# Another order for the filling work under the top-k search, and other steps for the down product's sums

## The chip, the cores and the metric

One core of a Trainium2 chip runs the whole kernel. The metric is the device time of one execution in microseconds (us); the profile is one further execution, read on the engines' own clocks.

## What is computed

One layer of a decoder trunk on x of 1024 tokens by 1024 channels, all in float32:

```python
h = x @ w_in + b_in                        # split into two groups of heads
A = sliding_window_attention(h)            # 8 q heads, 2 kv heads, window 128, sinks
B = sparse_attention(h)                    # indexer scores, top 256 keys, latent attention
x = LN(alpha * x + concat(A, B) @ w_o)
x = LN(alpha * x + cross_attention(x, mem))   # 4 heads over 256 memory tokens
x = LN(alpha * x + relu(x @ w_up) ** 2 @ w_down)
```

## The kernel before

A float32 product is made of three products on PE (TensorE), high by high, high by low and low by high. Each operand is split first: the high part is a rounding copy (ACT or POOL), the low part a subtraction (POOL or DVE, L166 and L1189).

**The fill.** From 149 us on, DVE and ACT search each row's threshold for the top 256 scores, and then DVE writes the masks (`mask_rows`, L820 to L830), 30 operations in six groups. PE has no part in this, so a list `fill` of other units is emitted beside it. A *projection* (`proj_unit`) is 24 products of 128x512 on the transposed x: ka (2 halves), qa (8), qb (8). Its result is split by ACT and DVE (L437, L438) and stored to DRAM by SP (L445). The other units: `mem_t` transposes the memory tokens; `lat` loads a latent weight and `latent_k` multiplies it (3 products); `mem_k` and `mem_v` are 24 products of 128x256 each; `mem_vo` multiplies by the output weight (12 products of 128x512 in each half). Each weight is loaded by SP into a ring of four raw tiles `wr`, split into a ring of four `wh`/`wl`. `open_attention` ends the life of the transposed x; the attention's operands (`KA`, from `first_loads`, L399) are put in its place, so no such load can be issued ahead of the last projection. The units before `CUT` are emitted ahead of `settle_all`, a branch that DVE takes after it has read a flag (`odd_row`, L754); the others follow it.

**The orders.** A scheduler fixes each engine's list of instructions when the program is built. An engine runs its list strictly in order, and SP issues loads and stores in its order too: a store that waits for DVE holds back every load behind it.

**The down product.** 28 of 32 row blocks of `w_down` are multiplied in a Strassen-like scheme of seven steps on quarters A11 to A22 and B11 to B22. `CHUNKS` runs three of them: 4 block pairs in the form `BACK`, 4 in `ONWARD`, 6 in `BACK`. A step's tuple names the sums of quarters it makes (DVE, L1435), the two quarters that it multiplies, and the additions of its results into `xr` (DVE, L1382, `out_add`). Of each pair of operands the high parts are copied by ACT (L1188) and the low parts are subtracted by DVE, or by POOL for three in eight (`lo_engine`, L1189). `AHEAD` keeps a sum from running more than five of DVE's subtractions ahead. The last four blocks are plain products, whose operands `in_slots` loads and splits (L1460 to L1462) into the places of quarters that are done.

Of the kernel before, what the change touches and what calls it, by code (L numbers as in the profile page):

```python
# [21 lines left out]
P = 128  # L22
KT = D // P
# [12 lines left out]
NOSYNC = mybir.DependencyInfo(mybir.DependencyClass.NoSync, mybir.DependencyReason.DATA)  # L36
# [3 lines left out]
def kernel(ctx: ExitStack, tc: tile.TileContext, x, mem, ln_emb_g, ln_emb_b, w_in, b_in,  # L40
# [449 lines left out]

    def mem_proj(c):
        if c % 2 == 0:
            FW["w"] = wload(xa_wkv, 0, KT, c * P, 256, lo=(POOL, DVE))
        wh, wl = cols(FW["w"], c % 2 * P)
        p = fill_bank()
        mm3(p[:, :M], [(wh[k], wl[k], memT[k // 4][:, k % 4, 0], memT[k // 4][:, k % 4, 1]) for k in range(KT)])
        return p[:, :M]
# [78 lines left out]
                W2[0] = qa, W2["bt"], qb, [bias_parts(e) for e in range(2)]  # L576

    qa, qb = [], []
    small = [(mem_t, mt, g) for mt in range(2) for g in range(2)] + [(lat, "uk", dsa_w_uk)]
    small += [(latent_k, j, t0, n) for j in range(4) for t0, n in HALVES] + [(lat, "uv", dsa_w_uv)]  # L580
    small += [(mem_k, c) for c in range(4)]
    heavy, fill = fill, []
    done = 0
    for i, u in enumerate(heavy):
        fill.append(u)
        want = i * len(small) // (len(heavy) - 1)
        fill += small[done:want]
        done = want
    fill += [(mem_k, c) for c in range(4, KT)]
    for h in range(4):  # L590
        fill += [(mem_v, h, d) for d in range(2)]
        if 0 < h < 3:
            fill += [(mem_vo, h - 1, nh) for nh in range(2)]
    fill.append((move_v,))
    for at, u in zip((13, 11, 10, 9, 8, 6, 5), [(open_attention,)] + [(first_loads, i) for i in range(6)]):
        fill.insert(len(fill) - at, u)

    CUT, MASKS = 26, 20
    ik = kdup(p1, ik_d, ("ikh",), ("ikl",))
    cm = p1.tile([P, P], F32, name="cm")  # L600
    DVE.memset(cm, 0.0)
# [231 lines left out]
    for unit, *args in fill[:CUT]:  # L833
        unit(*args)
    settle_all()
    for i, (unit, *args) in enumerate(fill[CUT:]):
        if i == MASKS:
            mask_rows()
        unit(*args)
    behind.clear()  # L840
    s1.close()
# [76 lines left out]
    def values(h0):  # L918
        vv = p2.tile([P, NB, 4, P], F32R, name="VV", bufs=1)
        us = slice(h0 * 64, h0 * 64 + 256)  # L920
        for s in range(0, NB, 2):
            p = psum.tile([P, 2, 256], F32, name="mm", bufs=2)
            for i in range(2):
                ts_ = slice((s + i) * P, (s + i) * P + P)
                mm3(p[:, i], [(cT[:, 0, ts_], cT[:, 1, ts_], uvh[:, us], uvl[:, us])])
            p_h = p.rearrange("p s (h d) -> p s h d", h=4)
            ACT.activation(vv[:, s:s + 2, :, 0:64], p_h, AF.Copy)
            DVE.tensor_tensor(out=vv[:, s:s + 2, :, 64:P], in0=p_h, in1=f(vv[:, s:s + 2, :, 0:64]), op=OP.subtract)
        return vv
# [327 lines left out]
    for j in range(1, NPRE):  # L1257
# [13 lines left out]
    A, B = OP.add, OP.subtract  # L1271
    ONWARD = (
        ((("B21", "B21", A, "B22"),), "A12", "B21", ((0, 0, A),), ()),
        ((("B12", "B12", A, "B11"),), "A21", "B12", ((1, 1, A),), ()),
        ((("AZ", "A11", A, "A22"), ("A21", "A21", A, "AZ")), "A21", "B11", ((1, 0, A), (1, 1, B)), ("A21",)),
        ((("A12", "A12", A, "AZ"),), "A12", "B22", ((0, 1, A), (0, 0, B)), ("A12",)),
        ((("B11", "B11", A, "B22"),), "AZ", "B11", ((0, 0, A), (1, 1, A)), ("AZ", "B22")),
        ((("B12", "B12", B, "B11"),), "A11", "B12", ((0, 1, A), (1, 1, A)), ("A11", "B12")),
# [1 line left out]
    BACK = (  # L1280
        ((("B21", "B21", B, "B11"),), "A22", "B21", ((0, 0, A), (1, 0, A)), ()),
        ((("B12", "B12", B, "B22"),), "A11", "B12", ((0, 1, A), (1, 1, A)), ()),
        ((), "A12", "B22", ((0, 1, A), (0, 0, B)), ()),
        ((), "A21", "B11", ((1, 0, A), (1, 1, B)), ()),
        ((("A11", "A11", A, "A22"), ("B11", "B11", A, "B22")), "A11", "B11", ((0, 0, A), (1, 1, A)), ("A22", "B22")),
        ((("A21", "A21", B, "A11"), ("B12", "B12", A, "B11")), "A21", "B12", ((1, 1, A),), ("A21", "B12")),
        ((("A12", "A12", B, "A11"), ("B21", "B21", A, "B11")), "A12", "B21", ((0, 0, A),), ("A12", "B21", "A11", "B11")))
    LOADS = {ONWARD: (("A12", "B21", "B22"), ("A21", "B12", "B11"), ("A11", "A22")),
             BACK: (("A22", "B21", "B11"), ("A11", "B12", "B22"), ("A12", "A21"))}

# [112 lines left out]
    for c, (r0, nk, steps) in enumerate(CHUNKS):  # L1403
        R, more, tags = {}, {}, {}

        def quarter(nm):

            t = free.pop(0)
            tags[nm] = [t]
            t = big(t, (P, 4, 512), F32)  # L1410
            R[nm] = [t[:, n] for n in range(4)]
            if nk > 4:
                pair = next(q for q in SHARED if nm in q)
                if pair not in more:
                    t = free.pop(0)
                    more[pair] = big(t, (P, 2, 2, 512), F32)
                    tags[pair] = [t]
                R[nm] += [more[pair][:, pair.index(nm), n] for n in range(2)]

        for names in LOADS[steps]:  # L1420
            for nm in names:
                quarter(nm)
            for n in range(nk):
                for nm in names:
                    SP.dma_start(R[nm][n], quarter_src(nm, r0 + 2 * n + int(nm[2 if nm[0] == "A" else 1]) - 1))
        if steps is ONWARD:
            quarter("AZ")
        for s, (sums, a, b, outs, done) in enumerate(steps):
            joined, open_ = c > 0 and s == 0, s == len(steps) - 1
            if not joined:  # L1430
                ps = [psum.tile([P, 512], F32, name=t, tag=t) for t in HALF[nst % 2]]
                nst += 1
            for n in range(nk):
                for o, x, op, y in sums:
                    i = DVE.tensor_tensor(out=R[o][n], in0=R[x][n], in1=R[y][n], op=op)  # L1435
                    if len(on_dve) > AHEAD:
                        tc.add_manual_dep(i.ins, on_dve[-1 - AHEAD].ins.name, NOSYNC, reason="order")
                ab = []
                for nm, w in ((a, WH), (b, WL)):
                    t = place(pw, w, [P, 2, 512], F32R)  # L1440
                    eng = lo_engine()
                    i = split(t, R[nm][n], eng)
                    if eng is DVE:
                        on_dve.append(i)
                    ab.append(t)
                for i in range(4):
                    ts_ = slice(i * P, i * P + P)
                    mm3(ps[i], [(ab[0][:, 0, ts_], ab[0][:, 1, ts_], ab[1][:, 0], ab[1][:, 1])],
                        n == 0 and not joined, n == nk - 1 and not open_)
            if not open_:  # L1450
                for i in range(4):
                    for t, d, op in outs:
                        out_add(ps[i], t * 4 + i, d, op)
            free += [t for q in (*done, *(q for q in more if set(q) <= set(done))) for t in tags[q]]
# [65 lines left out]
```

## Time and profile before

| | |
|---|---|
| median of three runs | 1546.09 us (1544.24 to 1546.13) |
| the profiled execution | 1550.19 us, its span 1548.4 us |
| PE busy | 1439.8 us (93%), mean granted clock 0.976 |
| PE weight loads | 1201.2 us (78%) |
| DVE, ACT, POOL busy | 1074.5 (69%), 754.0 (49%), 783.0 us (51%) |

A busy share is an average over all stages; a stage's own limit is read from the windows and the timelines of that stage. PE's clock is given as a share of full speed: 1.00 is 2.4 GHz, 0.50 is 1.2 GHz.

### The profile page before, as it was taken

How to read it: one execution, taken by the hardware profiler on the slowest of the kernel's cores; microseconds unless marked ns; L12 is line 12 of the kernel's file. 1: busy time of each engine (PE TensorE's matmuls, PEld its weight loads, DVE VectorE, ACT ScalarE, POOL GpSimd, SP SyncE). 2: the span in 40 equal slices, each digit the busy share in tenths (PEclk: the TensorE clock that was granted, in tenths of full speed). 3: DMA queues.
4: the chain of work that ended last, by engine and by line, in shares of the span. 5: the costliest groups of instructions: out<-in, count | busy, mean ns of one | idle time of the engine just before them, and what ended most of it. 6: DMA issues, size and time to landing. Idle time of an engine off the chain costs nothing. (4 is left out here: it accounts for less than half of the span.)

```text
span 1548.4 us, 21760 instructions
## 1 busy us (share of the span) xinstructions
PE 1439.8 (93%) x7190; PEld 1201.2 (78%) x7190; DVE 1074.5 (69%) x2060; ACT 754.0 (49%) x1517; POOL 783.0 (51%) x714
## 2 busy tenths in 40 slices
PE   4989998889989998999999889999999999999887
PEld 3977876768878876788888678888888877887676
DVE  6639888337769859883453775655444999978857
ACT  6437723447768844345153254455554543444422
POOL 6213433335548637566456575454443344354745
PEclk9999999989999999999999989999999999999899
DMA  6252544885595377333222134333334932410012
GB/s 220 67 166 62 164 123 131 281 267 149 160 262 161 113 227 225 123 109 107 85 83 89 41 116 150 103 123 109 109 109 157 374 104 95 155 55 0 28 35 102
DMA packets 140049, 206.62 MB, mean 133 GB/s; under 512 B 18199, under 2 KB 83230, under 8 KB 139934
## 3 DMA queue, kind: packets, MB, share of 16 engines
q1 hardware_dynamic: 139934, 205.21, 42.1%
q8 instruction: 57, 0.93, 0.3%
q14 instruction: 58, 0.48, 0.1%
HBM read 151.66 MB, written 52.45 MB: 132 GB/s over the span
## 5 line engine op out<-in xcount | busy, mean ns | idle before, releaser
L91 PE MATMUL b<-a,wh 128*128 128x512 f32 x1072 | 300.3, 402 | 9.1 <-DVE a L1175 7.9
L166 POOL TENSOR_TENSOR wl<-wr,wh 128x512 fp32r<-128x512 f32 x150 | 220.6, 1488 | 162.7 <-ACT wh L165 150.5
L91 PE MATMUL b<-wl,wh 128*128 128x512 f32 x1192 | 281.8, 396 | 14.0 <-POOL wl L1189 11.6
L91 PEld LDWEIGHTS b<-wl,wh 128*128 128x128 f32 x1192 | 227.0, 191 | 66.1 <-POOL wl L1189 14.4
L91 PEld LDWEIGHTS b<-a,wh 128*128 128x128 f32 x1072 | 204.1, 191 | 58.2 <-issue 8.7
L165 ACT ACTIVATE wh<-wr 128x512 fp32r<-128x512 f32 x144 | 85.5, 627 | 137.8 <-PE b L91 46.3
L1189 POOL TENSOR_TENSOR wl<-a,wl 128x512 fp32r<-128x512 f32 x44 | 91.2, 2072 | 115.2 <-ACT wl L1188 103.4
L1189 POOL TENSOR_TENSOR wh<-row,wh 128x512 fp32r<-128x512 f32 x72 | 97.5, 1358 | 91.0 <-ACT wh L1188 86.2
L91 PE MATMUL b<-wh,a 128*128 128x512 f32 (+1 forms) x416 | 122.2, 368 | 7.0 <-DVE a L859 5.3
L91 PE MATMUL fill<-xT,wh 128*128 128x512 f32 (+1 forms) x416 | 125.3, 380 | 1.2 <-ACT wt L441 0.8
L91 PE MATMUL b<-a,wl 128*128 128x512 f32 x400 | 123.1, 397 | 0.0
L1188 ACT ACTIVATE wh<-a 128x512 fp32r<-128x512 f32 x80 | 50.6, 633 | 115.6 <-PE b L91 84.2
L91 PEld LDWEIGHTS b<-wh,a 128*128 128x128 f32 x416 | 76.3, 191 | 22.5 <-DVE a L859 5.7
L1382 DVE TENSOR_TENSOR xr<-xr,b 128x512 f32<-128x512 f32 x132 | 81.4, 675 | 13.5 <-PE b L91 13.5
L91 PEld LDWEIGHTS fill<-xT,wh 128*128 128x128 f32 x416 | 76.3, 189 | 17.5 <-ACT wt L441 1.3
L91 PEld LDWEIGHTS b<-a,wl 128*128 128x128 f32 x400 | 75.2, 188 | 17.3
L1307 DVE TENSOR_TENSOR lt<-b,lt 128x512 f32<-128x512 f32 x80 | 53.4, 685 | 37.1 <-PE b L91 32.7
L91 PE MATMUL fill<-xT,wl 128*128 128x512 f32 (+1 forms) x208 | 78.7, 381 | 0.0
L867 DVE TENSOR_TENSOR PT<-tr,PT 128x512 fp32r<-128x512 f32 (+3 forms) x128 | 70.8, 575 | 11.1 <-ACT PT L866 10.6
L91 PE MATMUL b<-wl,a 128*128 128x512 f32 (+1 forms) x208 | 76.0, 368 | 1.2 <-POOL wl L166 1.2
L1188 ACT ACTIVATE wh<-row 128x512 fp32r<-128x512 f32 x72 | 45.0, 627 | 65.7 <-PE b L91 48.1
L866 ACT ACTIVATE PT<-tr 128x512 fp32r<-128x512 f32 (+3 forms) x128 | 61.9, 506 | 18.0 <-PE tr L968 12.3
(345 smaller groups left out, 3397.1 us busy)
## 6 DMA issues: line engine op xcount, KB each, us to landing
row<-in_w_up_dram SPq DMA_DIRECT2D x32, 512.0 KB, 3.7
ff_d<-lt SPq DMA_DIRECT2D x28, 512.0 KB, 3.7
a<-in_w_down_dram SPq DMA_DIRECT2D x50, 256.0 KB, 5.4
a<-ff_d SPq DMA_DIRECT2D x46, 256.0 KB, 4.2
wr<-in_xa_wkv_dram SPq DMA_DIRECT2D x32, 256.0 KB, 4.0
wr<-in_w_o_dram SPq DMA_DIRECT2D x32, 256.0 KB, 3.2
wr<-in_xa_wq_dram SPq DMA_DIRECT2D x32, 256.0 KB, 2.6
wr<-vwo_d SPq DMA_DIRECT2D x32, 256.0 KB, 2.7
```

Source lines behind the costliest of these rows:

```text
L91: i = PE.matmul(o, a, b, start=start, stop=stop)
L165: ACT.activation(hs, raw, AF.Copy)
L166: lo[i % len(lo)].tensor_tensor(out=ls, in0=raw, in1=f(hs), op=OP.subtract)
L866: ACT.activation(PT[0], pt, AF.Copy)
L867: DVE.tensor_tensor(out=PT[1], in0=pt, in1=f(PT[0]), op=OP.subtract)
L1188: ACT.activation(hl[:, 0], raw, AF.Copy)
L1189: return lo.tensor_tensor(out=hl[:, 1], in0=raw, in1=f(hl[:, 0]), op=OP.subtract)
L1307: DVE.tensor_tensor(out=o, in0=a, in1=b, op=op)
L1382: DVE.tensor_tensor(out=xs, in0=xs, in1=p, op=op)
```

## The change

Three things are edited. **First**, the fill's order: six projections (ka and half of qa) take all the small units among them, then mem_k 0 to 3 and the rest of qa stand ahead of `CUT`; behind it stand mem_k 4 to 7, qb among mem_v and mem_vo, then `open_attention` and the rest of the memory units with the first loads. The low parts of all `mem_k` weights are POOL's now, half of them were DVE's. **Second**, `mask_rows` follows the branch at once, where it stood 20 units later. **Third**, in the down product's `BACK` form the sum A11+A22 goes from step 4 to step 2, and A21-A11 from step 5 to step 3, where it follows two blocks behind the splits that read A21; in `ONWARD` the sum AZ goes from step 2 to step 1.

```diff
@@ -490,7 +490,7 @@
 
     def mem_proj(c):
         if c % 2 == 0:
-            FW["w"] = wload(xa_wkv, 0, KT, c * P, 256, lo=(POOL, DVE))
+            FW["w"] = wload(xa_wkv, 0, KT, c * P, 256, lo=(POOL,) if c < KT else (POOL, DVE))
         wh, wl = cols(FW["w"], c % 2 * P)
         p = fill_bank()
         mm3(p[:, :M], [(wh[k], wl[k], memT[k // 4][:, k % 4, 0], memT[k // 4][:, k % 4, 1]) for k in range(KT)])
@@ -576,26 +576,34 @@
                 W2[0] = qa, W2["bt"], qb, [bias_parts(e) for e in range(2)]
 
     qa, qb = [], []
+
     small = [(mem_t, mt, g) for mt in range(2) for g in range(2)] + [(lat, "uk", dsa_w_uk)]
     small += [(latent_k, j, t0, n) for j in range(4) for t0, n in HALVES] + [(lat, "uv", dsa_w_uv)]
-    small += [(mem_k, c) for c in range(4)]
+    keys = [(mem_k, c) for c in range(KT)]
+
+    def values(*hs):
+        return [(mem_v, h, d) for h in hs for d in range(2)]
+
+    def product(h):
+        return [(mem_vo, h, nh) for nh in range(2)]
+
     heavy, fill = fill, []
     done = 0
-    for i, u in enumerate(heavy):
+    for i, u in enumerate(heavy[:6]):
         fill.append(u)
-        want = i * len(small) // (len(heavy) - 1)
+        want = (i + 1) * len(small) // 6
         fill += small[done:want]
         done = want
-    fill += [(mem_k, c) for c in range(4, KT)]
-    for h in range(4):
-        fill += [(mem_v, h, d) for d in range(2)]
-        if 0 < h < 3:
-            fill += [(mem_vo, h - 1, nh) for nh in range(2)]
+    fill += keys[:4] + heavy[6:10]
+    CUT = len(fill)
+    fill += keys[4:] + heavy[10:14] + values(0) + heavy[14:15] + product(0) + heavy[15:]
+    tail = values(1, 2) + product(1) + values(3)
+    fill.append((open_attention,))
+    for i, u in enumerate(tail):
+        fill.append(u)
+        if i < 6:
+            fill.append((first_loads, i))
     fill.append((move_v,))
-    for at, u in zip((13, 11, 10, 9, 8, 6, 5), [(open_attention,)] + [(first_loads, i) for i in range(6)]):
-        fill.insert(len(fill) - at, u)
-
-    CUT, MASKS = 26, 20
     ik = kdup(p1, ik_d, ("ikh",), ("ikl",))
     cm = p1.tile([P, P], F32, name="cm")
     DVE.memset(cm, 0.0)
@@ -833,9 +841,8 @@
     for unit, *args in fill[:CUT]:
         unit(*args)
     settle_all()
-    for i, (unit, *args) in enumerate(fill[CUT:]):
-        if i == MASKS:
-            mask_rows()
+    mask_rows()
+    for unit, *args in fill[CUT:]:
         unit(*args)
     behind.clear()
     s1.close()
@@ -1271,8 +1278,8 @@
     A, B = OP.add, OP.subtract
     ONWARD = (
         ((("B21", "B21", A, "B22"),), "A12", "B21", ((0, 0, A),), ()),
-        ((("B12", "B12", A, "B11"),), "A21", "B12", ((1, 1, A),), ()),
-        ((("AZ", "A11", A, "A22"), ("A21", "A21", A, "AZ")), "A21", "B11", ((1, 0, A), (1, 1, B)), ("A21",)),
+        ((("B12", "B12", A, "B11"), ("AZ", "A11", A, "A22")), "A21", "B12", ((1, 1, A),), ()),
+        ((("A21", "A21", A, "AZ"),), "A21", "B11", ((1, 0, A), (1, 1, B)), ("A21",)),
         ((("A12", "A12", A, "AZ"),), "A12", "B22", ((0, 1, A), (0, 0, B)), ("A12",)),
         ((("B11", "B11", A, "B22"),), "AZ", "B11", ((0, 0, A), (1, 1, A)), ("AZ", "B22")),
         ((("B12", "B12", B, "B11"),), "A11", "B12", ((0, 1, A), (1, 1, A)), ("A11", "B12")),
@@ -1280,11 +1287,13 @@
     BACK = (
         ((("B21", "B21", B, "B11"),), "A22", "B21", ((0, 0, A), (1, 0, A)), ()),
         ((("B12", "B12", B, "B22"),), "A11", "B12", ((0, 1, A), (1, 1, A)), ()),
-        ((), "A12", "B22", ((0, 1, A), (0, 0, B)), ()),
+        ((("A11", "A11", A, "A22"),), "A12", "B22", ((0, 1, A), (0, 0, B)), ()),
         ((), "A21", "B11", ((1, 0, A), (1, 1, B)), ()),
-        ((("A11", "A11", A, "A22"), ("B11", "B11", A, "B22")), "A11", "B11", ((0, 0, A), (1, 1, A)), ("A22", "B22")),
-        ((("A21", "A21", B, "A11"), ("B12", "B12", A, "B11")), "A21", "B12", ((1, 1, A),), ("A21", "B12")),
+        ((("B11", "B11", A, "B22"),), "A11", "B11", ((0, 0, A), (1, 1, A)), ("A22", "B22")),
+        ((("B12", "B12", A, "B11"),), "A21", "B12", ((1, 1, A),), ("A21", "B12")),
         ((("A12", "A12", B, "A11"), ("B21", "B21", A, "B11")), "A12", "B21", ((0, 0, A),), ("A12", "B21", "A11", "B11")))
+
+    AFTER = {(BACK, 3): ("A21", "A21", B, "A11")}
     LOADS = {ONWARD: (("A12", "B21", "B22"), ("A21", "B12", "B11"), ("A11", "A22")),
              BACK: (("A22", "B21", "B11"), ("A11", "B12", "B22"), ("A12", "A21"))}
 
@@ -1430,11 +1439,17 @@
             if not joined:
                 ps = [psum.tile([P, 512], F32, name=t, tag=t) for t in HALF[nst % 2]]
                 nst += 1
+            def make(n, o, x, op, y):
+                i = DVE.tensor_tensor(out=R[o][n], in0=R[x][n], in1=R[y][n], op=op)
+                if len(on_dve) > AHEAD:
+                    tc.add_manual_dep(i.ins, on_dve[-1 - AHEAD].ins.name, NOSYNC, reason="order")
+
+            after = AFTER.get((steps, s))
             for n in range(nk):
-                for o, x, op, y in sums:
-                    i = DVE.tensor_tensor(out=R[o][n], in0=R[x][n], in1=R[y][n], op=op)
-                    if len(on_dve) > AHEAD:
-                        tc.add_manual_dep(i.ins, on_dve[-1 - AHEAD].ins.name, NOSYNC, reason="order")
+                for one in sums:
+                    make(n, *one)
+                if after and n > 1:
+                    make(n - 2, *after)
                 ab = []
                 for nm, w in ((a, WH), (b, WL)):
                     t = place(pw, w, [P, 2, 512], F32R)
@@ -1447,6 +1462,9 @@
                     ts_ = slice(i * P, i * P + P)
                     mm3(ps[i], [(ab[0][:, 0, ts_], ab[0][:, 1, ts_], ab[1][:, 0], ab[1][:, 1])],
                         n == 0 and not joined, n == nk - 1 and not open_)
+            if after:
+                for n in range(nk - 2, nk):
+                    make(n, *after)
             if not open_:
                 for i in range(4):
                     for t, d, op in outs:
```

SP's list behind the branch, before (`qb_d` and `kb_d` are stores of projections and of latent products, `wr` the loads of memory weights):

```order
L445 DMA qb_d_96<-wt_2384 64x2x512 x2
L445 DMA kb_d_97<-wt_2393 64x2x512 x2
L445 DMA qb_d_96<-wt_2425 64x2x512 x2
L445 DMA kb_d_97<-wt_2434 64x2x512 x2
L157 DMA wr_3446<-in_xa_wkv_dram 128x2x256
L157 DMA wr_3450<-in_xa_wkv_dram 128x2x256
L157 DMA wr_3456<-in_xa_wkv_dram 128x2x256
L157 DMA wr_3460<-in_xa_wkv_dram 128x2x256
```

and now (`wt_2445`, `wt_2475` and `wt_2505` are projections of qa; `wr_3443` to `wr_3457` are the weights of qb):

```order
L157 DMA wr_3381<-in_xa_wkv_dram 128x2x256
L445 DMA qa_d_95<-wt_2445 64x2x512 x2
L445 DMA qa_d_95<-wt_2475 64x2x512 x2
L445 DMA qa_d_95<-wt_2505 64x2x512 x2
L157 DMA wr_3443<-in_w_in_dram 128x2x256
L157 DMA wr_3447<-in_w_in_dram 128x2x256
L157 DMA wr_3453<-in_w_in_dram 128x2x256
L157 DMA wr_3457<-in_w_in_dram 128x2x256
```

The first weights behind the branch were those of `mem_k`, behind two stores of qb; now they are those of qb, behind three stores of qa. DVE splits `wt_2505` after the 21st of the 30 mask operations; before, `wt_2425`, the last store ahead of the loads, came after the 11th.

SP's list at the first loads for attention, before (`KAh`, `KAl`; `kT_d` are stores of `mem_k`, `wr` weights of `mem_v`):

```order
L157 DMA wr_3689<-in_xa_wkv_dram 128x2x256
L157 DMA wr_3693<-in_xa_wkv_dram 128x2x256
L503 DMA kT_d_90<-wt_3593 128x256
L399 DMA KAh_3751<-ka_d_94 64x1024 x2
L399 DMA KAl_3752<-ka_d_94 64x1024 x2
L503 DMA kT_d_90<-wt_3641 128x256
L157 DMA wr_3760<-in_xa_wkv_dram 128x2x256
```

and now (`wt_3851` is the last projection):

```order
L445 DMA qb_d_96<-wt_3791 64x2x512 x2
L445 DMA qb_d_96<-wt_3821 64x2x512 x2
L151 DMA wr_4026<-in_xa_wo_dram 128x512
L151 DMA wr_4030<-in_xa_wo_dram 128x512
L399 DMA KAh_3908<-ka_d_94 64x1024 x2
L399 DMA KAl_3909<-ka_d_94 64x1024 x2
L445 DMA qb_d_96<-wt_3851 64x2x512 x2
L404 DMA qs_3941<-qa_d_95 128x1024
L404 DMA qs_3991<-qa_d_95 128x1024
```

`KAh` stood far behind the last projection's store; now it stands ahead of that store, right behind the last projection's products. From it to the last `wl` load that attention's first wait needs, SP's list holds 50 transfers (14.3 MB by their shapes) before and 33 (10.2 MB) now.

DVE's list in the last chunk of the down product, where step 3 passes into step 4 (`a0` is A11, `a3` and `a4` B11, `a8` and `a9` A21, `a10` B12), before:

```order
L1435 TENSOR_TENSOR a0_13901<-a0_13901,a7_13878 128x512
L1435 TENSOR_TENSOR a3_13882<-a3_13882,a5_13905 128x512
L1189 TENSOR_TENSOR wh_14382<-a9_13904,wh_14382 128x512
L1189 TENSOR_TENSOR wl_14385<-a4_13881,wl_14385 128x512
L1435 TENSOR_TENSOR a0_13901<-a0_13901,a7_13878 128x512
L1435 TENSOR_TENSOR a3_13882<-a3_13882,a5_13905 128x512
L1189 TENSOR_TENSOR wh_14400<-a9_13904,wh_14400 128x512
L1435 TENSOR_TENSOR a1_13902<-a1_13902,fb0_13879 128x512 x2
L1435 TENSOR_TENSOR a4_13881<-a4_13881,fb0_13879 128x512 x2
L1462 TENSOR_TENSOR a5_14829<-wr_14838,a7_14828 128x512
L1462 TENSOR_TENSOR a5_14829<-wr_14842,a7_14828 128x512
L1189 TENSOR_TENSOR wh_14452<-a0_13901,wh_14452 128x512
```

and now:

```order
L1443 TENSOR_TENSOR a3_13882<-a3_13882,a5_13905 128x512
L1196 TENSOR_TENSOR wh_14391<-a9_13904,wh_14391 128x512
L1196 TENSOR_TENSOR wl_14394<-a4_13881,wl_14394 128x512
L1443 TENSOR_TENSOR a8_13925<-a8_13925,a0_13901 128x512
L1443 TENSOR_TENSOR a3_13882<-a3_13882,a5_13905 128x512
L1196 TENSOR_TENSOR wh_14410<-a9_13904,wh_14410 128x512
L1443 TENSOR_TENSOR a9_13904<-a9_13904,a1_13902 128x512
L1443 TENSOR_TENSOR a4_13881<-a4_13881,fb0_13879 128x512 x2
L1480 TENSOR_TENSOR a5_14829<-wr_14838,a7_14828 128x512
L1480 TENSOR_TENSOR a5_14829<-wr_14842,a7_14828 128x512
L1443 TENSOR_TENSOR a9_13904<-a9_13904,a1_13902 128x512
L1196 TENSOR_TENSOR wh_14462<-a0_13901,wh_14462 128x512
```

The sums on `a0` and `a1` (A11) have gone to an earlier place; those on `a8` and `a9` (A21), which came behind this piece, have taken theirs. The number of sums here is nearly the same.

## Rows read from the trace of the kernel before

**Rows 1.** Windows: us, then busy us (count) of PE, PEld, DVE, ACT, POOL, then PEclk, DMA share, GB/s

```profile
150.00:250.00 100.00, 98.78 (x433) 79.17 (x432) 84.61 (x234) 49.78 (x107) 38.47 (x36) 1.00 0.46 130
250.00:350.00 100.00, 77.63 (x484) 69.09 (x483) 48.68 (x62) 41.41 (x83) 34.37 (x29) 0.90 0.82 250
295.00:345.00 50.00, 43.14 (x279) 38.55 (x278) 17.12 (x25) 22.58 (x48) 17.35 (x17) 0.93 0.88 286
```

**Rows 2.** Waits of PE from 149 to 360: total, times, longest

```profile
PE fill L91 <- DVE wl L166: 7.5, 4, 5.5
PE lg L91 <- DMA wl<-kb_d: 4.4, 2, 3.4
```

**Rows 3.** Timeline of DVE from the search's end through the masks: start, us, operation

```profile
230.20 0.28 DVE L754 TENSOR_REDUCE some<-odd_row 1x1 int32<-1x128 f32 x1 [3.08 <-DMA odd_row<-odd]
...
236.86 0.42 DVE L826 TENSOR_SCALAR r<-sc,thr 128x384 f32<-128x384 f32 x1
...
256.10 1.74 DVE L166 TENSOR_TENSOR wl<-wr,wh 128x512 fp32r<-128x512 f32 x1
257.76 0.95 DVE L830 TENSOR_TENSOR sc<-r 128x768 f32<-128x768 f32 x1
...
268.41 0.74 DVE L438 SCALAR_TENSOR_TENSOR wt<-fill,colst,wt 128x512 fp32r<-128x512 f32 x1
```

**Rows 4.** Timeline of SP: the issue of one small load, then of stores

```profile
181.03 0.41 SPq L459 DMA_DIRECT2D wt<-in_dsa_w_uk_dram  x1
...
242.31 1.23 SPq L445 DMA_DIRECT2D qb_d<-wt  x2
```

**Rows 5.** Timeline of ACT: the first reader of the load issued at 181.03

```profile
184.38 0.63 ACT L461 ACTIVATE wt<-wt 128x512 fp32r<-128x512 f32 x1 [0.41 <-DMA wt<-in_dsa_w_uk_dram]
```

**Rows 6.** Timeline of POOL: weight splits before and inside the masks

```profile
178.05 1.20 POOL L161 TENSOR_SCALAR wh<-wr 128x512 fp32r<-128x512 f32 x2 [11.62 <-PE fill L91]
179.21 2.55 POOL L166 TENSOR_TENSOR wl<-wr,wh 128x512 fp32r<-128x512 f32 x2
...
248.69 4.54 POOL L166 TENSOR_TENSOR wl<-wr,wh 128x512 fp32r<-128x512 f32 x2
```

**Rows 7.** Windows of a projection, of a mem_k after a wait, of the same later; columns as before

```profile
182.65:188.25 5.60, 5.60 (x25) 4.51 (x24) 5.39 (x21) 5.19 (x13) 4.04 (x4) 1.00 0.98 282
258.27:261.47 3.20, 3.20 (x16) 3.20 (x16) 3.20 (x4) 0.00 (x0) 0.00 (x0) 0.50 0.52 164
262.47:264.63 2.16, 2.16 (x21) 2.16 (x20) 2.16 (x4) 1.16 (x2) 0.66 (x1) 1.00 0.84 249
```

**Rows 8.** Timeline of SP: the first of the loads for attention

```profile
294.98 1.14 SPq L399 DMA_DIRECT2D KAh<-ka_d  x2
```

**Rows 9.** Timeline of PE: attention's wait for the last of them

```profile
349.56 0.44 PE L91 MATMUL lg<-wl,qs 128*128 128x128 f32 x1 [3.41 <-DMA wl<-kb_d]
```

**Rows 10.** Windows of the down product, columns as before

```profile
1245.00:1250.00 5.00, 5.00 (x24) 4.14 (x23) 5.00 (x9) 1.79 (x4) 0.07 (x1) 1.00 0.03 11
1270.00:1290.00 20.00, 17.00 (x66) 12.91 (x65) 20.00 (x27) 6.13 (x11) 7.56 (x6) 0.91 0.78 260
1430.00:1445.00 15.00, 8.43 (x26) 6.40 (x25) 9.09 (x15) 5.58 (x11) 10.04 (x6) 0.66 0.21 70
1470.00:1480.00 10.00, 6.05 (x20) 4.17 (x19) 3.65 (x7) 1.68 (x3) 8.89 (x5) 0.83 0.07 26
```

**Rows 11.** Timeline of POOL in the down product: two splits

```profile
1425.93 8.83 POOL L1462 TENSOR_TENSOR a<-wr,a 128x512 fp32r<-128x512 f32 x2 [4.30 <-ACT a L1461]
...
1462.85 11.44 POOL L1189 TENSOR_TENSOR wl<-a,wl 128x512 fp32r<-128x512 f32 x1 [1.65 <-ACT wl L1188]
```

**Rows 12.** Timeline of DVE in the same stretch

```profile
1420.40 1.77 DVE L1189 TENSOR_TENSOR wl<-a,wl 128x512 fp32r<-128x512 f32 x1
...
1432.34 1.27 DVE L1382 TENSOR_TENSOR xr<-xr,b 128x512 f32<-128x512 f32 x2
...
1472.48 0.67 DVE L1189 TENSOR_TENSOR wl<-a,wl 128x512 fp32r<-128x512 f32 x1
```

## The prediction

> **What bounds the kernel now.** I read the windows by stage first, since PE is busy for 93% of the span and only its idle stretches can be won. Under the search, from 150 to 250 us, it is busy for 98.78 of 100; from 250 to 350 for 77.63, at clock 0.90 [rows 1]. Then the waits: PE's waits for low parts on DVE sum to 7.5 us, 5.5 at once, and attention's two waits for `kb_d` to 4.4 [rows 2]. The timeline of DVE shows why: one weight's low part (256.10, 1.74 us) stands among the masks [rows 3]. In the down product three stretches are thin: 66 products start from 1270 to 1290, where 24 in 5 us are full speed, 26 from 1430 to 1445, 20 from 1470 to 1480 [rows 10]. That is 30, 46 and 28 products less than 96, 72 and 48; at 5/24 us each 6.3, 9.6 and 5.8 us, 21.7 in all. The reader should see two prizes: 22.4 us of idle PE in the fill and 21.7 us in the down product.
>
> **The fill, part by part.** The products are the same, so only idle time changes. I walk from what fixes the end backwards.
>
> *Small units early.* SP's list now has the load of `w_uk` behind the first qa store, and PE has nothing else until the latent products. Such a load took 3.4 us from issue to its first reader (181.03 to 184.38) [rows 4, 5]; with ACT's and POOL's split behind it I put PE's idle time at some 8 us, and at as much again for the two qa halves that wait for DVE's low parts among the search's passes. I let this cost nothing, and name the cover: PE's units ahead of qb are nine halves of 24 wide products from 149 on, 25 of which start in 5.60 us [rows 7], so 5.6 us a half or 50 us, eight `mem_k` of half the columns, some 2.9 each, 23 us, and 8 us for the latent products and transposes. They end at 230 without idle time and at 254 with all I can find, and what follows waits for 267 anyway.
>
> *Masks at once.* In both orders DVE reaches the masks when the flag has landed (230.20) and the branch is taken: 236.86 now [rows 3]. SP's list has the flag's store behind one more weight load, which waits for POOL; I take 239, with 231 (no wait behind the flag) and 242 as ends.
>
> *POOL's eight low parts.* They leave DVE's list (1.74 us of it ahead of the 21st mask operation) and PE's 5.5 us wait goes. POOL runs them in the same stretch in which it took 4.54 us for two, against 2.55 outside it [rows 3, 6]. I take no further cost, since `mem_k` 6 and 7 are covered by the same wait as above.
>
> *qb's weights.* This is the term that decides. SP issues them behind the store of `wt_2505`, which DVE splits after the 21st mask operation. That operation ended at 257.76 + 0.95, so 21.9 us behind the masks' start; less the 1.74 it is 20.2 [rows 3]. From 239 this gives 259.2; the split takes 0.74 (that of 268.41), two stores 1.23 as at 242.31 [rows 3, 4], the load 3.4, POOL's two high parts 1.20 and two low parts 2.55 [rows 6], of which PE needs the first half to start. So qb begins at about 267.5, and PE stands idle for 13 us or more ahead of it. That SP is held back by a store behind the masks is no new thing: the store of 242.31 was also the first issue after the masks' start. Next come eight halves (44.8 us), two `mem_v` (5.8) and 24 wide products of `mem_vo` (5.6), 56.2 us. After a wait PE's clock is low: 16 products in 3.20 us at 0.50 against 21 in 2.16 at 1.00 [rows 7], so 1.6 us more. The last projection ends at about 325.
>
> *The loads for attention.* They can't be issued before that, as they go into the place of x. Before, the first was issued at 294.98 [rows 8], and the last product of attention's first wait began at 349.56 [rows 9]: 14.3 MB in 54.6 us, 262 GB/s, while PE still had its own work. Now 10.2 MB stand between, and PE has only 23 us of memory units left beside them (six `mem_v`, 17.4, and one `mem_vo` pair, 5.6), so DMA is the bound. The busiest 50 us of before moved 286 GB/s at a share of 0.88 [rows 1]; I take 286, so 36 us, with 325 (286/0.88, an estimate) and 262 as ends, 31 and 39 us. Attention's wait then ends at 361, 11.5 us later than 349.6.
>
> Ends of this part: masks at 231 (-8) and DMA at 325 (-4) give about -1; masks at 242 (+3), POOL's splits twice as long under the masks (+3) and 262 GB/s (+3) give +21.
>
> **The down product.** Two POOL subtractions took 8.83 us and one 11.44 [rows 11]; alone a pair takes 2.55 [rows 6]. The second began at 1462.85 and ended 1.1 us after DVE's run of subtractions and sums ended (1472.48 + 0.67); the first ended after DVE had gone over to additions from PSUM (1432.34) [rows 11, 12]. When POOL has begun first, DVE's operation grows from 0.67 to 1.77 us [rows 12]. So a POOL operation waits for a gap in a run of DVE operations on two SBUF operands. The Trainium skill, "SBUF — State Buffer", section "SBUF: two separate sides", says that whichever of the two starts first holds the shared ports for the whole instruction and that the other blocks. The 1.77 agrees; the 11.44 does not, as by that rule POOL would wait for one instruction, 0.67 us at most, and sums in other places would win nothing here (the sum would be 1550.2 + 11.5).
>
> What the sums' move does to the runs: in the first chunk steps 4 to 6 have 16 sums where they had 24, 8 at some 0.63 (1.27 for two [rows 12]) or 5 us less work on a DVE that was busy for all 20 us from 1270 to 1290 [rows 10]; but it is busy for all of 1245 to 1250 too, where the sums go, so I take 3 of the 6.3 us. In the last chunk the run at step 3's end keeps nearly all its operations (ten in a row in place of thirteen) and POOL's two subtractions of plain operands still stand in front of step 4's: nothing of the 9.6. In step 4 six sums go, which lets DVE enter step 5 earlier, but step 5's own run is as long and POOL now has one subtraction more ahead of the one that PE waited for: 1.5 of the 5.8. Sum -4.5, ends 0 and -12 (both outer stretches wholly won). The sum AZ stands where PE doesn't wait: nothing.
>
> **The sum.** 1550.2 + 11.5 - 4.5 = 1557.2 for the profiled execution, which is 4.1 above the median of the runs; against that median, 1546.1 + 7 = 1553.
>
> **The rivals.**
> - *The locked runs break.* If the moved sums open one gap in each of the three runs, POOL's subtractions fall back to some 1.3 us, and 17 of the 21.7 us come back. For it: each run ended a wait only at its very end [rows 11, 12]. Against it: DVE's list at step 3's end. It decides from the point where POOL's pair of plain operands takes under 4 us. 1546.1 + 11.5 - 17 = 1541, faster. 0.18.
> - *The fill's idle time goes and nothing takes its place.* qb's weights would have to come by 254, and the loads for attention to hide under PE's work. Then 14 of the 22.4 us come back: 1546.1 - 14 - 4.5 = 1528. The masks' place in DVE's list speaks against it. 0.12.
> - *DMA runs at full share and the masks start as before.* -2 and -4 on the fill's 11.5 leave +5, the down product takes them back: 1547. 0.13. The Trainium skill, "DMA: Bandwidth & Descriptors", section "Bandwidth", puts one core's limit to HBM at some 358 GB/s; by it the 10.2 MB would take 28 us, an estimate, and the sum would be 1545.
> - *The upper end.* The early idle time also holds up ACT's part of the search and POOL's splits are slow: +21 - 2, 1565. 0.10.
> - *My forecast*, the rest: 0.47, by its own ends 1537 to 1567.
>
> **How the numbers follow.** No change means within 0.2% (3.1 us), about what a measurement of this kernel can tell. Faster hold the first two rivals and a little of the third and of the forecast's lower end: 0.32. The same: most of the third and the forecast's edge, 0.12. Slower: 0.56. For 8 in 10 I leave out the second rival and the tails of the others: 1536 to 1568. The likeliest case by itself, slower, is 1549 to 1567.
>
> **What would show it.** Right: PE without a wait on DVE's `wl` at 250 to 258; an idle gap of over 8 us ahead of qb's first half, ended by POOL's split; the first `KAh` issue at 315 to 330 in place of 294.98, and a DMA share over 0.9 behind it; attention's first `kb_d` wait ending at 355 to 367; POOL's two plain subtractions still at 6 us or more. Wrong: qb beginning by 256, or attention's wait ending before 350, would refute the fill's part; POOL without any operation over 5 us in the down product would refute the second.

## The result, and the profile after

The median went from 1546.09 to 1554.71 us (1550.20 to 1556.24), a ratio of 1.0051, 95% interval [1.0034, 1.0068]: slower by 8.6 us where 7 was forecast (1553, range 1536 to 1568). The profiled execution of the changed kernel, 1550.20 us, is the fastest of its seven, that of before one of its slower ones; both have a span of 1548.4 us, so the loss is not read from the two spans but from the stages.

Windows of after (us, busy us and count of PE, PEld, DVE, ACT, POOL, PEclk, DMA share, GB/s):

```profile
150.00:250.00 100.00, 86.70 (x448) 72.11 (x447) 90.82 (x232) 57.71 (x122) 49.88 (x40) 0.93 0.49 136
250.00:350.00 100.00, 87.29 (x469) 73.25 (x467) 40.85 (x49) 30.33 (x55) 35.93 (x33) 0.95 0.73 224
1270.00:1290.00 20.00, 20.00 (x90) 16.53 (x89) 20.00 (x30) 8.65 (x16) 9.40 (x7) 1.00 0.78 262
1430.00:1450.00 20.00, 18.80 (x79) 14.28 (x78) 20.00 (x28) 10.47 (x19) 10.39 (x8) 1.00 0.11 37
```

Beside [rows 1], PE's idle time has moved: 12 us more of it under the search, 10 less from 250 to 350. Beside [rows 10], the thin stretch at 1270 is full.

Waits of PE, after, 149 to 400 (total, times, longest):

```profile
PE fill L91 <- POOL wh L161: 8.8, 1, 8.8
PE fill L91 <- ACT wt L461: 6.8, 1, 6.8
PE fill L91 <- ACT wt L441: 5.4, 3, 3.9
PE lg L91 <- DMA wh<-kb_d: 5.1, 1, 5.1
PE lg L91 <- DMA wl<-kb_d: 3.0, 2, 2.4
```

The wait on DVE's low parts [rows 2] is gone. In its place: 12.2 us at the latent weights' products (L461, L441), 8.8 for POOL's split of qb's first weights, and a longer wait at attention. The chain behind the 8.8 us, in the timelines of DVE, SP, POOL and PE of after (start, us, operation, idle time before):

```profile
232.12 0.42 DVE L834 TENSOR_SCALAR r<-sc,thr 128x384 f32<-128x384 f32 x1
...
252.29 0.74 DVE L438 SCALAR_TENSOR_TENSOR wt<-fill,colst,wt 128x512 fp32r<-128x512 f32 x1
```

```profile
237.57 16.72 SPq L445 DMA_DIRECT2D qa_d<-wt  x6
254.38 2.81 SPq L157 DMA_DIRECT2D wr<-in_w_in_dram  x4
...
322.07 1.14 SPq L399 DMA_DIRECT2D KAh<-ka_d  x2
```

```profile
259.02 0.93 POOL L161 TENSOR_SCALAR wh<-wr 128x512 fp32r<-128x512 f32 x1 [15.67 <-DMA wr<-in_w_in_dram]
```

```profile
260.00 1.22 PE L91 MATMUL fill<-xT,wh 128*128 128x512 f32 x2 [8.79 <-POOL wh L161]
...
356.09 0.77 PE L91 MATMUL lg<-wh,qs 128*128 128x128 f32 x2 [5.06 <-DMA wh<-kb_d]
358.09 0.45 PE L91 MATMUL lg<-wl,qs 128*128 128x128 f32 x1 [0.59 <-DMA wl<-kb_d]
```

The masks begin at 232.12. SP stands in its list of six qa stores for 16.72 us, until DVE has split the third of qa's last four halves (252.29, among the masks), and only then issues qb's weights. PE begins qb at 260.00; `KAh` is issued at 322.07, and attention's first wait ends at 358.09, 8.5 us later than [rows 9].

The down product gives part of it back. From its first product to the end of the span it took 342.2 us before (1206.20 to 1548.4) and 336.8 after (1211.56 to 1548.4). The remaining 3 us between the two profiles lie between the end of that wait and the down product, in code that neither edit touches: 853.5 us in this execution, 855.5 to 856.6 in the profiles of before, e1 and e2 (853.0 to 861.9 in all the profiles below).

### The profile page after: what moved, and what is told of

Same layout as the page of the kernel before. It is cut to its first block, busy times and chain, and to the rows that moved or that the text cites. A ratio compares the mean times of both kernels' runs of the same rounds, so it can differ in the third digit from the quotient of the medians.

```text
span 1548.4 us, 21751 instructions
## 1 busy us (share of the span) xinstructions
PE 1434.5 (93%) x7190; PEld 1196.2 (77%) x7190; DVE 1085.9 (70%) x2052; ACT 754.6 (49%) x1517; POOL 782.7 (51%) x722
## 5 line engine op out<-in xcount | busy, mean ns | idle before, releaser
L166 POOL TENSOR_TENSOR wl<-wr,wh 128x512 fp32r<-128x512 f32 x158 | 229.5, 1473 | 162.0 <-ACT wh L165 153.8
L91 PE MATMUL b<-wl,wh 128*128 128x512 f32 x1192 | 277.6, 392 | 12.9 <-POOL wl L1196 7.1
L91 PEld LDWEIGHTS b<-wl,wh 128*128 128x128 f32 x1192 | 223.9, 188 | 64.0 <-POOL wl L1196 8.4
L91 PE MATMUL fill<-xT,wh 128*128 128x512 f32 (+1 forms) x416 | 128.5, 388 | 9.7 <-POOL wh L161 8.8
L1196 POOL TENSOR_TENSOR wl<-a,wl 128x512 fp32r<-128x512 f32 x44 | 71.7, 1629 | 109.3 <-ACT wl L1195 92.1
L91 PEld LDWEIGHTS b<-wh,a 128*128 128x128 f32 x416 | 75.6, 190 | 20.2 <-ACT a L865 3.3
L1316 DVE TENSOR_TENSOR lt<-b,lt 128x512 f32<-128x512 f32 x80 | 53.4, 687 | 36.6 <-PE b L91 31.7
L873 ACT ACTIVATE PT<-tr 128x512 fp32r<-128x512 f32 (+3 forms) x128 | 61.9, 507 | 21.7 <-PE tr L975 11.8
```

The source lines that it names most:

```text
L91: i = PE.matmul(o, a, b, start=start, stop=stop)
L166: lo[i % len(lo)].tensor_tensor(out=ls, in0=raw, in1=f(hs), op=OP.subtract)
L873: ACT.activation(PT[0], pt, AF.Copy)
L1196: return lo.tensor_tensor(out=hl[:, 1], in0=raw, in1=f(hl[:, 0]), op=OP.subtract)
L1316: DVE.tensor_tensor(out=o, in0=a, in1=b, op=op)
```

## The experiments

All were timed in five rounds beside the kernel before on the same chip; ratios are against that. "After" is the changed kernel.

**The two halves of the change.** e1 keeps the fill and undoes the down product; e2 the reverse.

```diff
e1, on the changed kernel (and its loop as before)
-        ((("A11", "A11", A, "A22"),), "A12", "B22", ((0, 1, A), (0, 0, B)), ()),
+        ((), "A12", "B22", ((0, 1, A), (0, 0, B)), ()),
...
-    AFTER = {(BACK, 3): ("A21", "A21", B, "A11")}
e2, on the kernel before: the third part of the change alone
```

> The change's fill alone, with the down product of before. Theory (the fill costs by late loads of qb's weights and of attention's operands, the down product gives back some 4.5 us): attention's first wait ends 7 to 12 us later than before, the median is 1557 to 1560, slower than the whole change. Rival 1 (the down product's edit does nothing, the fill is the whole loss): 1554 to 1556. Rival 2 (the down product costs and the fill is nearly level): 1550 or less.

> The change's down product alone, with the fill of before. Theory: 3 to 6 us faster than before, 1540 to 1543; the first chunk loses under 1.5 us to waits (4.7 before), POOL's two plain subtractions stay over 6 us. Rival 1: no difference, 1545 to 1547. Rival 2: slower, 1549 or more.

Measured: e1 1557.82 us, 1.0075 [1.0049, 1.0100]; e2 1540.06, 0.9962 [0.9946, 0.9978]. Both theories held: the fill costs some 11.6 us, the down product gives 5.9, together 1.0037, inside the change's interval. e2 beats both kernels. One line of e2's expectation missed: POOL's pair of plain subtractions fell to 3.38 us instead of staying over 6. Attention's first wait ended at 357.7 in e1; with the fill of before at 349.6 in before's profile, and at 346.0, 347.7 and 347.3 in e2, e3 and e8. So the fill's cost at that place is some 8 to 12 us.

The second edit by itself was not run: with `mask_rows` emitted ten or twenty units later the scheduler gives every engine the same list, so the loss is not its doing.

**The sum AZ** (e3: e2 with AZ back in step 2).

```diff
-        ((("B12", "B12", A, "B11"), ("AZ", "A11", A, "A22")), "A21", "B12", ((1, 1, A),), ()),
-        ((("A21", "A21", A, "AZ"),), "A21", "B11", ((1, 0, A), (1, 1, B)), ("A21",)),
+        ((("B12", "B12", A, "B11"),), "A21", "B12", ((1, 1, A),), ()),
+        ((("AZ", "A11", A, "A22"), ("A21", "A21", A, "AZ")), "A21", "B11", ((1, 0, A), (1, 1, B)), ("A21",)),
```

> As the run before, but the sum AZ of the ONWARD form stays in step 2, as in the kernel before. If the early AZ is what made PE wait for 1.5 us in the second chunk's first step, this run is 1 to 2 us faster than the one with it; if that wait comes from the sums B21 and B12 there, the two are the same within 1 us.

Measured: 1539.86 us, 0.9959 [0.9942, 0.9975]. In the trace `ONWARD`'s first step takes 10.88 us again in place of 12.36 (e2), so the sum's move costs 1.5 us there; the medians, 0.2 apart, don't show it.

**POOL's plain subtractions** (e8: e2 with all of them on DVE).

```diff
-            lo_engine().tensor_tensor(out=l[:, n], in0=raw, in1=f(h[:, n]), op=OP.subtract)
+            DVE.tensor_tensor(out=l[:, n], in0=raw, in1=f(h[:, n]), op=OP.subtract)
```

> The change's down product on the fill of before, with all low parts of the last four plain blocks subtracted by DVE; POOL had six of the 16. Theory (a POOL subtraction waits for a gap in DVE's run, and PE for the POOL subtractions queued behind it): POOL's 10 us operation in step 5 goes and with it most of PE's wait there, 3 to 5 us less than the run without this edit, 1535 to 1537. Rival (DVE is full there, six more operations of 0.6 us push its run out): the same or up to 3 us more, 1540 to 1543.

Measured: 1540.79 us, 0.9972 [0.9960, 0.9985], no gain. The long POOL operation is still there and longer; only its name has changed. Timelines of POOL, DVE and PE of e8:

```profile
1448.25 15.46 POOL L1189 TENSOR_TENSOR wh<-fb,wh 128x512 fp32r<-128x512 f32 x1 [0.94 <-ACT wh L1188]
```

```profile
1447.46 0.69 DVE L1189 TENSOR_TENSOR wh<-a,wh 128x512 fp32r<-128x512 f32 x1
...
1461.90 0.70 DVE L1473 TENSOR_TENSOR a<-wr,a 128x512 fp32r<-128x512 f32 x1
```

```profile
1464.99 10.31 PE L91 MATMUL b<-wl,wh 128*128 128x512 f32 x38 [9.07 <-POOL wl L1189]
```

DVE ran 25 operations on two SBUF operands from 1447.46 to 1462.60 without a gap. POOL's one subtraction began during the second, lasted through the rest and ended 1.1 us after the last. The rival (DVE is full there) held: what was taken off POOL made DVE's run longer.

**POOL's eight low parts of the keys' weights** (e12: e2 with that part of the fill's edit).

```diff
-            FW["w"] = wload(xa_wkv, 0, KT, c * P, 256, lo=(POOL, DVE))
+            FW["w"] = wload(xa_wkv, 0, KT, c * P, 256, lo=(POOL,) if c < KT else (POOL, DVE))
```

> The kernel before's filling work with the changed down product, in which the low parts of the split columns of the first chunks go to POOL alone instead of alternately to POOL and VectorE. Theory (TensorE's wait of 7.5 us on VectorE's low parts is there because VectorE, which also carries the sums, is the later of the two): the wait on VectorE goes, POOL's stays under 6 us in sum, and the kernel is 3 to 6 us faster than the same kernel with the parts shared, 1534 to 1537. Rival (POOL becomes the later one, or the product is bound by the sums of its last steps): no difference beyond 2 us, 1538 to 1542, with a wait on POOL's low parts in place of VectorE's.

The text on record names the wrong place: these low parts and the 7.5 us wait [rows 2] belong to the fill, not to the down product. Its first sentence on the wait still applies, as the waits of PE from 149 to 400 show, in e2:

```profile
PE fill L91 <- DVE wl L166: 7.2, 3, 5.4
```

and in e12:

```profile
PE fill L91 <- DVE wt L438: 8.5, 2, 7.9
```

The wait is gone and another of 7.9 us, for a projection's split on DVE, stands in its place. Measured: 1543.56 us, 0.9980 [0.9965, 0.9994]; the theory failed, nothing is gained over e2.

**qa ahead of the keys** (e6), **qb ahead of the values** (e5), **both** (e7).

```diff
e6
-    fill += keys[:4] + heavy[6:10]
+    fill += heavy[6:10] + keys[:4]
e5
-    fill += keys[4:] + heavy[10:14] + values(0) + heavy[14:15] + product(0) + heavy[15:]
+    fill += keys[4:] + heavy[10:] + values(0) + product(0)
```

> The whole change, but the four halves of qa stand ahead of mem_k 0 to 3, so that their stores are issued ahead of the branch and SP has no store that waits for the masks when it comes to qb's weights. Theory: qb's first half begins at 250 to 253 in place of 260, PE's 8.8 us wait ahead of it goes, the first KAh load is issued at 311 to 316, attention's first wait ends 6 to 9 us earlier, the median is 1546 to 1549. Rival (the masks and POOL's splits under them set qb's start, whatever the order of SP): less than 3 us, 1552 to 1556.

> The whole change, but behind the branch mem_k 4 to 7 and all eight halves of qb stand ahead of mem_v 0 and mem_vo 0. SP then issues the first attention load some 11 us earlier (at 311 in place of 322), with 10.6 MB in place of 10.2 up to attention's first wait. Theory (that wait ends some 36 us behind the first load, set by DMA): it ends at 347 to 351 in place of 358, the median is 7 to 10 us below the whole change, 1545 to 1548. Rival (the wait is set by PE's and POOL's own work on the memory units, which is the same): it ends at 355 or later, the median within 3 us of the whole change.

> The two orders together: qa ahead of mem_k 0 to 3, and all of qb ahead of mem_v 0 and mem_vo 0. Theory: first attention load at 306 to 309, attention's first wait ends at 343 to 346, the median is 1539 to 1543, level with the change's down product on the fill of before (1540.06) or better. Rival (one of the two covers the other): as the better of the two alone, 1545 or more.

**w_uk earlier** (e9), **all of qa split ahead of the masks** (e10), **e9 and e6 together** (e13).

```diff
e9
+    small.insert(2, small.pop(4))
e10: each mask operation's place on DVE behind qa's last split
+            tc.add_manual_dep(i.ins, qsplit[-1].ins.name, NOSYNC, reason="order")
```

> The whole change, but the latent weight w_uk is loaded two units earlier, ahead of the first qa store. Theory: PE's wait of 6.8 us at 164 to 171 for ACT's copy of it goes, and nothing is won, as qb's start is set by the masks: qb's first half still begins at 258 to 262, the median within 2 us of the whole change. Rival (the early idle time carries through to the end): 5 to 7 us faster, 1548 to 1550.

> The changed kernel with one thing changed: VectorE makes all four last-half subtractions of qa (L438) before it begins the masks; the early placing of the memory's products stays, with its waits on ScalarE. Theory (after's loss in the filling work is that SP's queue holds qb's weights behind the store of qa's last half, which is 7 mask operations late on VectorE): the masks start about 243 us instead of 232, qb's weights are issued at 244 to 247 instead of 254.4, qb begins at 249 to 252 instead of 260, the last projection ends near 311, the loads of the attention begin near 312 and its wait ends 36 us later, at 347 to 350 instead of 358; some 9 us less than the changed kernel at the end, 1544 to 1548. Rival (the masks now lie under qb's first products, whose halves VectorE and POOL must split, and delay them by what the weights gained): the last projection ends at 317 or later, the wait at 354 or later, 1552 or more.

> The changed kernel with w_uk's load and split earlier among the small units, and the last four halves of qa ahead of the first four products of the memory's keys. Theory (the changed kernel's loss is how long after the masks' start SP comes to qb's weights, and each of these two edits took some of it away for itself: 11 us and 7 us): the last projection ends at 303 to 307 and the loads of the attention begin there, its wait ends 36 to 37 us later, at 340 to 344, which is 2 to 5 us earlier than in the kernel before's order; with the down product's gain of 5 us the median is 1535 to 1540. Rival (qa earlier means that VectorE and ScalarE, still in the search, split it later than TensorE makes it, and the masks start later: the gain of the second edit is not there when the first is in): the wait ends at 345 or later, 1542 to 1546.

What these kernels showed, each from its timelines (start of the masks on DVE, of SP's issue of qb's weights, of qb's first and last product on PE, of the `KAh` issue, of the product that ends attention's first wait; in e5 and e7 PE does not wait there, and the column has its first product on `kb_d`) and its times:

| | masks | weights | qb from | to | KAh | wait ends | median | ratio |
|---|---|---|---|---|---|---|---|---|
| after | 232.1 | 254.4 | 260.0 | 321.2 | 322.1 | 358.1 | 1554.71 | 1.0051 |
| e5 | 234.7 | 256.7 | 262.3 | 312.2 | 317.6 | 360.1 | 1556.94 | 1.0073 [1.0051, 1.0096] |
| e6 | 239.8 | 241.1 | 248.4 | 317.6 | 318.5 | 355.3 | 1547.98 | 1.0014 [0.9993, 1.0034] |
| e7 | 241.6 | 242.9 | 250.2 | 294.8 | 307.0 | 346.6 | 1544.85 | 0.9995 [0.9981, 1.0008] |
| e9 | 233.7 | 240.0 | 246.1 | 308.0 | 308.9 | 345.5 | 1543.68 | 0.9986 [0.9970, 1.0002] |
| e10 | 241.8 | 238.6 | 250.9 | 315.8 | 316.7 | 353.6 | 1549.22 | 1.0020 [1.0002, 1.0038] |
| e13 | 243.3 | 239.8 | 247.4 | 318.5 | 319.4 | 355.8 | 1552.93 | 1.0041 [1.0025, 1.0058] |

Three readings. *First*, most of the time is carried by the end of attention's wait: 13 to 15 us between e9 and after or e5 come back as 11 to 13 in the medians. It does not carry all of it: e13 and e6 reach that product at 355.8 and 355.3, e7 and e2 at 346.6 and 346.0, and the ratios of each pair are some 0.3% apart (the intervals of e7 and e2 don't overlap). From that product to PE's first product behind attention (into `b`) it takes 205 to 208 us in e5, e7, e9 and e13 and 201 to 205 in the others; it begins at 562.6 in e13 and 558.2 in e6, at 554.5 in e7 and 548.9 in e2. What lengthens that stretch was not tested.

*Second*, from `KAh` to that end it takes 36.0 us in after, 36.8 in e6, 36.6 in e9, 36.9 in e10, 36.4 in e13: the loads bound it. The window of that stretch in after has a DMA share of 1.04, where before had 0.90 from 294.98 to 349.56:

```profile
322.07:358.09 36.02, 28.89 (x201) 25.66 (x201) 13.60 (x27) 15.57 (x35) 13.48 (x17) 0.96 1.04 315
```

Where qb is made earlier without the memory's weights (e5, e7), 42.5 and 39.6 pass, since those weights now stand among the attention's loads. PE then has no wait for `kb_d`; it waits for ACT's split of a memory weight, which waits for that weight. Timelines of ACT and PE of e5:

```profile
341.17 1.28 ACT L165 ACTIVATE wh<-wr 128x512 fp32r<-128x512 f32 x2 [3.84 <-DMA wr<-in_xa_wo_dram]
```

```profile
341.86 2.07 PE L91 MATMUL fill<-wh,wt 128*128 128x512 f32 x4 [5.86 <-ACT wh L165]
```

`KAh` itself came 5 and 12 us behind the last projection. So e5's theory failed and its rival held; e7, with both edits, missed its theory's 1539 to 1543 and is back at the time of before and no further; e6's median came as its theory had it, though its trace stands between theory and rival, with new waits (5.6 us for ACT's split at 238.6, 3.0 for DVE's low parts at 274.9) in the place of the 8.8.

*Third*, qb's beginning is not enough. With weights issued 13 to 16 us earlier, qb's last product came 13 us earlier in e9, but 3 to 5 in e6, e10 and e13, where 65 to 71 us in place of 61 pass from first to last.

e9 refuted my theory, by which the early idle time has a cover. It made the kernel 0.65% faster than after (0.9986 to 1.0051, some 10 us), more than its rival's 5 to 7. Timelines of SP and DVE of e9:

```profile
223.22 0.55 SPq L756 DMA_DIRECT2D odd_row<-odd  x1
223.96 15.95 SPq L445 DMA_DIRECT2D qa_d<-wt  x6
240.01 3.79 SPq L157 DMA_DIRECT2D wr<-in_w_in_dram  x4
```

```profile
237.92 0.74 DVE L438 SCALAR_TENSOR_TENSOR wt<-fill,colst,wt 128x512 fp32r<-128x512 f32 x1
```

The split that holds SP stands behind the 7th mask operation instead of the 21st, so the weights come 14.4 us earlier. The edit moved both: PE was idle 7.5 us from 150 to 200 (12.4 in after), and DVE's list, which is fixed at build, was another. e10 keeps after's early idle time (11.0 us) and changes DVE's list alone (the lists of PE, ACT and POOL stay, two entries of SP's swap places): the weights come at 238.6, as early as in e9, and the kernel is 0.3% faster than after (1.0020 to 1.0051, the intervals just overlap), about half of e9's gain and between its own theory and rival; attention's wait ends 4.5 us earlier. So the split's place is very likely a cause by itself, worth some 5 us.

The traces show where the rest of e9's gain lies. In e10 PE begins qb without a wait, right behind its own earlier units:

```profile
250.87 0.63 PE L91 MATMUL fill<-xT,wh 128*128 128x512 f32 x2
```

With the weights there in time, it is PE's own work with the early idle time in it that sets qb's start, 4.8 us later than in e9. Those earlier units end at 251.0 in e10 and at 242.2 in e9: up to there PE is idle for 11.8 and 7.5 us, and from 150 to 200 its granted clock is 0.83 and 0.93. Another 3.0 us are lost in qb's stretch, where the memory's products wait 4.6 us for ACT's splits; the masks lie 8 us later than in e9. What each of the two is worth in the kernel's time was not run alone.

e13 failed both theory and rival in its time: two edits, each a gain, together keep almost nothing (1.0041 to 1.0051). The rival had the direction, masks that start later. Timelines of SP and DVE of e13:

```profile
226.07 4.88 SPq L445 DMA_DIRECT2D qa_d<-wt  x6
231.05 1.07 SPq L756 DMA_DIRECT2D odd_row<-odd  x1
...
239.83 3.96 SPq L157 DMA_DIRECT2D wr<-in_w_in_dram  x4
```

```profile
242.45 0.97 DVE L829 TENSOR_SCALAR ngt<-ngt 128x6 f32<-128x6 f32 x1 [8.02 <-DMA wr<-in_w_in_dram]
```

Timelines of DVE, e9 and then e13, the operation that makes the flag:

```profile
223.05 0.14 DVE L754 TENSOR_SCALAR odd<-odd 128x1 f32<-128x1 f32 x1
```

```profile
229.98 0.14 DVE L754 TENSOR_SCALAR odd<-odd 128x1 f32<-128x1 f32 x1
```

In e13 DVE has eight of the projections' splits between 149 us and the flag, where e9 has four, and is idle there for 4 us more; it makes the flag 6.9 us later. The six stores of qa, which now stand ahead of the flag's store (231.05, in e9 223.22), add less than 1 us to that. DVE takes the branch later and the masks begin 10 us later. That the masks, under which POOL and DVE then split the memory's weights, stretch qb from 62 to 71 us was seen in the waits (4.7 us on ACT, 2.6 on DVE's low parts, both on memory weights), but no run isolates it.

The best versions are those with the fill of before: e2 and e3, 0.9962 and 0.9959.

## Why the prediction was right

*The term that decides* was right in place and size, not in its start. Masks: 239 forecast, 232.1 measured (the low end was 231), because SP stored the flag at 222.69, as soon as DVE had made it; before, the store came 3.2 us after that (226.55). From the masks' start to the split that holds SP: 20.2 forecast, 20.2 measured (252.29 less 232.12). From that split to qb's first product: 8.3 and 7.7. So qb began at 260.0 in place of 267.5. PE's earlier units ended at 251.2, so its idle time ahead of qb was 8.8 us and not 13 or more. (The two early idle times that the prediction names make 246 with its 230; its 254 is not worked out.)

*qb and the memory units*: 57.5 us forecast, 61.2 measured; two waits for POOL's low parts, of 1.4 and 1.0 us, are in it. The last projection came at 321 (325 forecast).

*The loads*: 36 us forecast, 36.0 measured, and 36.4 to 36.9 in four more kernels: the firmest term. By the Trainium skill, "DMA: Bandwidth & Descriptors", section "Bandwidth" (some 358 GB/s a core), it would have been 28, an estimate; no run here came near that, though from 330 to 340 us after moved 390 GB/s by the window's count, more than that limit, and 315 over the whole stretch. The sign, a DMA share over 0.9 behind `KAh`, held (1.04). Attention's wait ended at 358.1 for 361.

*The step that failed* is the cover of the early idle time: "I let this cost nothing". It reasoned with DVE's list as given, and in that list it holds, for at 252.29 DVE took the split without waiting. But that list was built from the same order of units: e9 moved one early unit and got the loads of qb 14 us earlier. What the early order costs is thus, for some 5 of the 10 us, its effect on the list, which I had not looked for (e10). Much of the rest is that the cover is gone as soon as qb's weights come in time: in e10 PE's own units, with the early idle time in them, set qb's start.

*The down product* was right in its sum (-4.5; some -5.4 between the traces, 5.9 us by e2) and wrong in its parts; that the sum came out is luck. (Its full rate, 24 products in 5 us, counts products that only touch the window; a step of 48 without waits takes 10.88 us. By steps the three stretches held 5.8, 9.6 and 6.2 us, close to its 6.3, 9.6 and 5.8.) First chunk: 3 of 6.3 forecast, 5.8 won (81.9 to 76.2 us from its first product to the next chunk's), as its steps run without a wait. `ONWARD`'s AZ: nothing forecast, 1.5 lost (e3). Step 4 of the last chunk: nothing forecast, but 18.7 us from its start to the next in place of 25.9, 7.2 won; step 5: 1.5 won forecast, 4.0 lost (26.5 for 22.5). From step 6 to the end of the span another 2.1 are lost (72.5 for 70.4). Together that is the 5.4. The rows that answer to [rows 11] and [rows 12], timeline of POOL, then of DVE:

```profile
1425.28 3.38 POOL L1480 TENSOR_TENSOR a<-wr,a 128x512 fp32r<-128x512 f32 x2 [2.44 <-DVE a L1443]
...
1459.47 10.02 POOL L1480 TENSOR_TENSOR a<-wr,fb 128x512 fp32r<-128x512 f32 x1 [8.48 <-issue]
1469.46 1.25 POOL L1196 TENSOR_TENSOR wl<-a,wl 128x512 fp32r<-128x512 f32 x1
```

```profile
1425.72 1.79 DVE L1443 TENSOR_TENSOR a<-a,a 128x512 f32<-128x512 f32 x1
...
1458.65 0.69 DVE L1196 TENSOR_TENSOR wh<-a,wh 128x512 fp32r<-128x512 f32 x1
...
1465.88 2.50 DVE L1443 TENSOR_TENSOR a<-a 128x512 f32<-128x512 f32 x4
```

The pair that took 8.83 takes 3.38, so my sign "6 us or more" was wrong, and the first rival (the locked runs break) happened in two of the three: in the first chunk too POOL's longest operation fell from 4.44 us to 1.75. The last run stayed locked, 16 operations from 1458.65 on, POOL's 10.02 us through all but the first.

That rival had the wrong price. Its 1541 had the fill's loss in it, so that loss is not why it did not come: of its 17 us only 5.4 came back. Two runs show that the last lock is not what was missing. In e10 and e12 the lists of DVE, ACT and POOL in the down product are those of after, and yet POOL got in at the same place. Timelines of POOL and DVE of e10:

```profile
1458.24 1.62 POOL L1483 TENSOR_TENSOR a<-wr,fb 128x512 fp32r<-128x512 f32 x1 [8.47 <-issue]
```

```profile
1458.63 1.77 DVE L1446 TENSOR_TENSOR fb<-fb,a 128x512 f32<-128x512 f32 x1
```

POOL's 10.02 us became 1.62, but DVE's operations grew, and PE waited for DVE's splits instead (9.2 us from 1449 on; in after 10.6, of which 6.8 for POOL's). From its first product to the end of the span the down product took 335.6 us in both, 1.2 less than after: with all three runs broken 6.6 us came back (8.1 without AZ's loss), not 17.

## What to carry to other kernels

Moving units in a list that feeds a scheduler moves more than those units: look where the splits and stores of the moved results come to stand on the engine that is busy and on the DMA queue, ahead of or behind the flag, the branch and the next loads. When a bound at the end of a stage is a block of loads (36 us here), count the time from the issue that starts them, and judge a reordering by that issue and by what it puts among the loads (e5 had the issue earlier and lost). Test the parts of a change apart: here one half was a gain of 0.4% under a loss of 0.75%.

## What was unexpected of the hardware

A POOL subtraction can last to the end of a run of DVE operations on two SBUF operands that has no gap: 10.02 us through the last 15 of 16 (after), 15.46 us through the last 24 of 25 (e8), each ending 1.1 us after the run. Elsewhere the two alternate: at 1425.72 DVE's operation grew to 1.79 us while POOL's took 1.7 each. The Trainium skill, "SBUF — State Buffer", section "SBUF: two separate sides", has the loser wait for the other's whole instruction; the 1.79 agrees, the 15.46 doesn't. In both cases POOL began while a DVE operation was running. The order of the lists does not decide it either: with the same lists, and begun 0.21 us after the start of the same DVE operation, the same POOL subtraction took 10.02 us in after and 1.62 in e10. What lets it in stays open.
